# Waiting for a buffer's readers, and one addition for all deferred evictions, in a one-core hybrid trunk step

## The chip, the cores and the metric

The kernel runs as one program on one core of a Trainium2 chip. The time is the device time of one execution in microseconds (us); less is better. The engines are TensorE (PE: matmuls into eight banks of PSUM), VectorE (DVE), ScalarE (ACT), GpSimd (POOL) and SyncE (SP), whose queue issues nearly all of the DMAs.

## The reference

One inference step of a two-layer diffusion trunk over 128 context and 512 latent positions, 640 columns, with model width 2048. Each layer modulates and normalises x, multiplies by one wide input weight, runs two mixers on the halves, gates them, multiplies by an output weight and adds the result to x. The even layer has windowed attention with a sink and a gated linear scan (GLA); the odd layer has attention over a two-dimensional neighbourhood and a chunked spatial-gating MLP (gMLP).

```python
# one layer, shapes cut
m = silu(cond) @ w_ada + b_ada                 # shift, scale, gate
h = (rms_norm(x, g) * (1 + scale) + shift) @ w_in
parts = split_cols(h, SPLITS)
mix = concat(branch_a(parts), branch_b(parts)) # window attention | GLA, or 2-D attention | gMLP
x = x + gate * ((mix * silu(parts[-1])) @ w_out)
# after two layers
y = rms_norm(x, g_final)
```

All inputs and outputs are float32, and the caches and the GLA state of the context are outputs too.

## The kernel before

**Products.** Activations lie transposed, feature blocks of 128 on the partitions and 640 positions along a row, each as a high part (acth) and a low part (actl). A weight block of 128x512 is loaded as float32 into a raw buffer (wraw or rs), copied by ACT into its high half (whi, half a microsecond or so), and POOL or DVE subtracts that from the raw block to get the low half (wlo). Every product of a weight block with an activation block is three matmuls: whi with the high part, whi with the low part, wlo with the high part (`three`).

**Strassen pairs.** From the out-projection of layer 0 on, two output chunks are computed together in a pair of Winograd's form (`spair`): seven products of quarter matrices in place of eight, on sums of activations that a `fold` prepares. `fold` runs once for the odd layer's input (about 1075 to 1270 us) and once for the last out-projection (about 1900 to 2010 us), between chunks computed in the plain way. Its near half (`work`) writes the sums into SBUF as eh and el and the third operand over t3_dram; its far half (`far`) makes them in place on POOL and ACT, in Y, adas and one shared buffer `stage`, and stores them to far_dram. From there they come back as "tail" slots (`far_load`), small buffers through which the far products read them. `third` loads the third operand, t_dram in the profile, back over acth and actl when their first use is over. `keep` saves what is overwritten and `unfold` brings it back.

**Partial sums.** A product that several outputs share stays in a bank. `copy` has ACT copy it into the SBUF buffer `sums`, of which there is one, and DVE adds `sums` to each output's bank. These additions and the evictions behind them are not issued at once: `later` puts a generator into the list `evq`, and `deferred` (called by `tick`, between matmuls) takes steps of the first generator of the list when its time has come. An eviction (`ev`) first waits for flags that its chunk needs, such as home8, which is set when an attention head is done.

**What sets the order.** There is no reordering on the chip: each engine runs its instructions as they were written. The program is written by `tick`, which runs tasks (generators) between matmuls, and by a planner (`Pace`), which models when each engine and each DMA will be done. `until(...)` holds a task until the planner thinks that a buffer has been written. It doesn't ask for those who still read the buffer; if a step overwrites a buffer too soon, the engine waits on the chip for the reader's semaphore, and all that stands behind it on that engine waits too. `settle` exhausts all generators in `evq` at once, with `force` set: then no task's wait holds, and a flag that is missing is reached by running the tasks until it is there (`need`). `copy` calls it since the addition that reads `sums` has to be written before `sums` is overwritten.

**Places that the prediction names.** All ACT, DVE and POOL steps go through one helper and have line L208, all DMAs of SP L428; the matmuls have L394 (products) and L399 (transposes with ident). `tail<-bank` at 1078 us is the eviction of an output tile of layer 0 (`out_evac`), whose closing step `end` squares the tile for the norm; `Y` and `arena` are working buffers of the attention heads, and `adas` holds ada weights early and tiles of the mixers' output late.

## Time and profile before

| what | value |
| --- | --- |
| median of 3 runs | 2150.63 us (2147.55 to 2153.57) |
| the profiled execution's own time | 2151.12 us |
| its span | 2149.3 us |
| mean granted clock of PE | 0.992 |
| POOL wlo<-wraw and wlo<-rs, 128x512 | 341 of 1403 ns and 275 of 1444 ns |
| ACT whi<-wraw and whi<-rs | 397 and 329 of 623 ns |
| SP tail<-far_dram | 196 loads of 322 KB, 4.2 us to landing |

The span is the time from the first to the last instruction of the profiled execution; 1.8 us of the execution lie around it. In a row of the timeline stand the start, the length, the engine, the line, the operation, output and inputs, and in brackets how long the engine had been idle before it and what ended that. PE's idle time is what to look for, as PE is the busy engine; idle time of other engines matters where PE waits for them.

### The profile page before, as it was taken

Reading aid. Unit: us, or ns where it says so; the run is one execution under the profiler, and the core shown is the slowest. Engines: PE = TensorE matmul, PEld = TensorE weight load, DVE = VectorE, ACT = ScalarE, POOL = GpSimd, SP = SyncE. Lnnn points to the kernel's source line nnn. Section 1 sums busy time; section 2 is a strip of 40 time slices with the busy share of each in tenths; the row PEclk is TensorE's granted clock in tenths of the full one; section 3 lists DMA queues with packets and bytes.
Section 4 is the critical chain, followed back from the end, with each engine's and each line's share of the span. In section 5 each row is a group of like instructions: output and inputs, shape, how many; then the busy total and the mean of one; then the engine's idle time right before and its main releaser. Section 6 shows DMA issues by size and latency. Waiting matters only on the chain. (4 is left out here: it accounts for less than half of the span.)

```text
span 2149.3 us, 38899 instructions
## 1 busy us (share of the span) xinstructions
PE 2069.3 (96%) x13990; PEld 1985.7 (92%) x13990; DVE 1533.2 (71%) x3383; ACT 964.8 (45%) x2100; POOL 1033.0 (48%) x781
## 2 busy tenths in 40 slices
PE   7999999999999999999989999999999999999896
PEld 5789999999989999999989999999999989999896
DVE  1337777777887866788766898878778767665565
ACT  3335444343433445433554434545454544444343
POOL 3433333223313222455465666746556556656773
PEclk9999999999999999999999999999999999999998
DMA  9955333336545433866557766656666565565756
GB/s 368 324 181 162 125 106 105 104 127 189 158 119 173 141 125 102 259 217 219 156 184 243 232 217 227 230 183 212 210 216 194 189 232 194 195 222 184 242 191 218
DMA packets 216306, 412.48 MB, mean 192 GB/s; under 512 B 25712, under 2 KB 89008, under 8 KB 216112
## 3 DMA queue, kind: packets, MB, share of 16 engines
q1 hardware_dynamic: 214640, 408.43, 57.9%
q8 instruction: 110, 1.80, 0.3%
q10 hardware_dynamic: 1472, 1.56, 0.2%
q14 instruction: 84, 0.69, 0.1%
HBM read 368.83 MB, written 38.45 MB: 189 GB/s over the span
## 5 line engine op out<-in xcount | busy, mean ns | idle before, releaser
L394 PE MATMUL bank<-acth,whi 128*128 128x320 f32 (+1 forms) x3144 | 965.9, 319 | 20.9 <-ACT whi L208 8.1
L394 PE MATMUL bank<-acth,wlo 128*128 128x320 f32 (+1 forms) x3144 | 941.9, 311 | 9.7 <-POOL wlo L208 8.8
L394 PE MATMUL bank<-actl,whi 128*128 128x320 f32 (+1 forms) x3144 | 939.2, 310 | 0.0
L208 POOL TENSOR_TENSOR wlo<-wraw,whi 128x512 fp32r<-128x512 f32 x345 | 480.3, 1399 | 749.5 <-ACT whi L208 648.3
L394 PEld LDWEIGHTS bank<-acth,whi 128*128 128x128 f32 x3144 | 584.5, 189 | 41.2 <-ACT whi L208 10.8
L394 PEld LDWEIGHTS bank<-acth,wlo 128*128 128x128 f32 x3144 | 584.1, 189 | 14.8 <-POOL wlo L208 13.2
L394 PEld LDWEIGHTS bank<-actl,whi 128*128 128x128 f32 x3144 | 584.7, 189 | 1.5
L208 POOL TENSOR_TENSOR wlo<-rs,whi 128x512 fp32r<-128x512 f32 x275 | 393.4, 1444 | 238.3 <-ACT whi L208 196.4
L208 ACT ACTIVATE whi<-wraw 128x512 fp32r<-128x512 f32 (+1 forms) x397 | 242.6, 623 | 161.3 <-PE bank L394 84.5
L208 ACT ACTIVATE whi<-rs 128x512 fp32r<-128x512 f32 x329 | 197.6, 623 | 57.9 <-PE bank L394 35.3
L208 DVE CUSTOM_DVE_ANT_0 adas<-adas,bank,partg 128x256 bf16<-128x256 f32 (+1 forms) x320 | 178.1, 557 | 14.8 <-DMA adas<-ada_g 5.0
L394 PE MATMUL bank<-tail,whi 128*128 128x322 f32 (+1 forms) x672 | 152.5, 314 | 6.6 <-DMA tail<-far_dram 6.5
L394 PE MATMUL bank<-eh,whi 128*128 128x322 f32 (+1 forms) x444 | 139.8, 315 | 0.0
L394 PE MATMUL bank<-eh,wlo 128*128 128x322 f32 (+1 forms) x444 | 138.5, 312 | 1.0 <-POOL wlo L208 1.0
L394 PE MATMUL bank<-el,whi 128*128 128x322 f32 (+1 forms) x444 | 138.0, 311 | 0.0
L208 ACT ACTIVATE bc<-bank 128x2 f32<-128x2 f32 (+1 forms) x101 | 17.2, 170 | 230.9 <-DVE arena L208 153.6
L394 PEld LDWEIGHTS bank<-tail,whi 128*128 128x128 f32 x672 | 112.5, 189 | 7.4 <-DMA tail<-far_dram 7.4
L208 ACT ACTIVATE Y<-bank 128x128 f32<-128x128 f32 (+5 forms) x134 | 52.6, 412 | 140.2 <-PE bank L394 82.2
L394 PE MATMUL bank<-tail,wlo 128*128 128x322 f32 (+1 forms) x336 | 104.4, 311 | 0.2 <-POOL wlo L208 0.2
L208 DVE TENSOR_TENSOR bank<-bank,sums 128x320 f32<-128x320 f32 (+1 forms) x162 | 76.5, 493 | 36.7 <-PE bank L394 28.9
L208 ACT ACTIVATE arena<-arena,bc 128x192 f32<-128x192 f32 (+4 forms) x167 | 82.3, 517 | 42.6 <-DVE arena L208 40.9
L208 DVE TENSOR_TENSOR rs<-rs 128x512 f32<-128x512 f32 x83 | 84.4, 1025 | 21.2 <-POOL wlo L208 20.5
(215 smaller groups left out, 2928.1 us busy)
## 6 DMA issues: line engine op xcount, KB each, us to landing
tail<-far_dram SPq DMA_DIRECT2D x196, 322.0 KB, 4.2
wraw<-w_even SPq DMA_DIRECT2D x176, 256.0 KB, 3.3
adas<-ada_g SPq DMA_DIRECT2D x128, 256.0 KB, 4.2
adas<-ada SPq DMA_DIRECT2D x128, 256.0 KB, 3.6
rs<-w_odd SPq DMA_DIRECT2D x63, 512.0 KB, 5.4
Y<-ada SPq DMA_DIRECT2D x37, 512.0 KB, 5.8
wraw<-w_odd SPq DMA_DIRECT2D x37, 512.0 KB, 5.4
rs<-w_out SPq DMA_DIRECT2D x30, 512.0 KB, 5.0
```

The lines of the kernel that those rows point to most:

```text
L208: return f(*args, **kw)
L394: self.nc.tensor.matmul(out, lhsT, rhs, start=start, stop=stop, **kw)
```

## The change

Three edits, all to when a step is written and none to what it computes.

1. `clear` now asks the planner when the engine could run a step that writes `outs` and reads `ins`, readers of `outs` included, and holds the task until that is no more than 0.1 us ahead, and until no DMA that the planner holds for late touches them. It is called before the ACT copy of the near half's split (new) and of the far half's split (before: without the engine and with a looser rule), before the closing step of an output tile (before: `until`) and before the scaling of Y's tiles (`scales`).
2. `copy`, and the step of a plain block that starts the output ya, call `release` in place of `settle`. The list `xq` holds the deferred generators that still have to read `sums`; `release` forces each of them up to its addition (`used_up` takes it off the list), and what follows, the eviction, stays deferred.
3. `third` waits, ahead of its first far block, until the tail slots have been loaded.

```diff
-    def clear(self, *aps):
-
-        spans = [self.pace.span(x) for x in aps]
-        while not self.force and (self.left(*aps) > 0.05 or any(self.pace.meet(x[1], spans) for x in self.pace.late)):
-            yield 0.5
+    def clear(self, e, outs, ins=()):
+
+        pc = self.pace
+        o, i = [pc.span(x) for x in outs], [pc.span(x) for x in ins]
+        while not self.force:
+            if any(pc.meet(x[1], o) or pc.meet(x[1][:1], i) for x in pc.late):
+                yield 0.5
+                continue
+            w = pc.ready(e, o, i) - self.now
+            if w <= 0.1:
+                return
+            yield w
...
+    def release(self):
+
+        while self.xq:
+            item = self.xq[0]
+            was, self.force, self.busy = (self.force, self.busy), True, True
+            try:
+                next(item[1])
+            except StopIteration:
+                self.evq.remove(item)
+            self.force, self.busy = was
...
         def copy(a):
-            self.settle()
+            self.release()
             x = self.sums[:, : a.shape[1]]
             nc.scalar.activation(x, a, AF.Copy)
             return x
...
-        def later(c, gen):
+        def later(c, gen, x=True):
             self.evq.append([self.now, gen, c])
+            if x:
+                self.xq.append(self.evq[-1])
+
+        def used_up():
+            self.xq.pop(0)
+            yield
 
         def one(xa, x):
             yield from self.until(x)
             plus(full(xa), x)
+            yield from used_up()
             yield from ev(c1, xa, None)
             self.drop(xa)
...
                     ya = ya or take()
-                    self.settle()
+                    self.release()
                     plain(key, ya, v)
...
         def split(h, l, p):
+            yield from self.clear("a", [h], [p])
             nc.scalar.activation(h, p, AF.Copy)
...
-                yield from self.clear(h, x)
+                yield from self.clear('a', [h], [x])
                 h, l = h.bitcast(F32R), x.bitcast(F32R)
...
                 yield from self.wait("Tn" if i < NR else "Tf", f"{used if i < NR else far_used}:{i}")
+                if i == NR:
+                    yield from self.until(*self.slots)
                 for n, x in enumerate((self.ah, self.al)):
...
             def end(c):
-                yield from self.until(y[:, c], self.sq)
+                yield from self.clear('a', [self.sq], [y[:, c]])
                 square(y, c)
...
-                yield from self.clear(Y[:, k, :])
+                yield from self.clear('a', [Y[:, k, :]])
```

The numbers of instructions are the same on every engine but for 16 subtractions wlo that move from DVE to POOL. PE's order is the same up to about 1095 us (in the first fold); after that only small matmuls (attention, transposes, sums over partitions) and a few plain blocks stand elsewhere between the weight products.

**ACT in the second fold (about 1926 to 1942 us).** Before; Y<-Y, Y<-adas and stage<-adas are the far half's copies, arena<-Y is a step of the gates, whi the weights' high halves:

```order
L208 ACTIVATE Y<-Y 128x320
L208 ACTIVATE stage_7782<-adas 128x320
L208 ACTIVATE whi<-rs_7781 128x512 x2
L208 ACTIVATE Y<-adas 128x320
L208 ACTIVATE stage_7782<-adas 128x320
L208 ACTIVATE arena_7788<-Y 128x320 x4
L208 ACTIVATE sums_7784<-bank_69 128x320
L208 ACTIVATE whi<-wraw 128x512 x2
L208 ACTIVATE whi<-rs_7781 128x512 x2
```

And with the change, the rows that stand there:

```order
L208 ACTIVATE stage_7782<-adas 128x320
L208 ACTIVATE whi<-rs_7781 128x512
L208 ACTIVATE Y<-Y 128x320
L208 ACTIVATE whi<-wraw 128x512
L208 ACTIVATE arena_7788<-Y 128x320 x2
L208 ACTIVATE whi<-wraw 128x512
L208 ACTIVATE arena_7788<-Y 128x320 x2
L208 ACTIVATE stage_7782<-adas 128x320
L208 ACTIVATE sums_7784<-bank_70 128x320
L208 ACTIVATE whi<-rs_7781 128x512
L208 ACTIVATE Y<-adas 128x320
```

The two weight copies whi<-wraw stood behind both overwriting steps with adas, the four gate steps and the copy into sums; one of them now stands ahead of the gate steps and one between them, and the step Y<-adas that followed the first stage<-adas stands behind them all.

**PE at the end of attention head 7 (1726 us).** The bank that PE's products with Y write is filled from transposes (ident). Before:

```order
L399 MATMUL bank_72<-ident,Y 128x128 x3
L399 MATMUL bank_73<-ident,arena_7788 128x128
L399 MATMUL bank_73<-ident,arena_7788 64x128
L399 MATMUL bank_73<-ident,arena_7788 128x128
L394 MATMUL bank_72<-Y 128x512
L394 MATMUL bank_72<-Y 128x128
L394 MATMUL bank_72<-Y 128x256 x3
L394 MATMUL bank_72<-Y 128x128
L394 MATMUL bank_69<-acth,whi 128x320
L394 MATMUL bank_69<-actl,whi 128x320
L394 MATMUL bank_69<-acth,wlo 128x320
```

With the change, the two places, first behind the first transposes, then ahead of the products with Y (the rows between are weight products like those shown):

```order
L399 MATMUL bank_72<-ident,Y 128x128 x3
L394 MATMUL bank_69<-acth,whi 128x320
L394 MATMUL bank_69<-actl,whi 128x320
L394 MATMUL bank_69<-acth,wlo 128x320
L394 MATMUL bank_69<-acth,whi 128x320
```

```order
L399 MATMUL bank_73<-ident,arena_7788 128x128
L399 MATMUL bank_73<-ident,arena_7788 64x128
L399 MATMUL bank_73<-ident,arena_7788 128x128
L394 MATMUL bank_71<-eh_7779,whi 128x322
L394 MATMUL bank_71<-el_7780,whi 128x322
L394 MATMUL bank_71<-eh_7779,wlo 128x322
L394 MATMUL bank_71<-eh_7779,whi 128x322
```

The second group of transposes stood directly behind the first and the products with Y directly behind the second; now 18 weight products stand between the two groups, and 18 between the second group and the products with Y.

**SP at the end of the second fold (about 1990 to 2007 us).** Before:

```order
L428 DMA tail_19307<-far_dram 128x2x320
L428 DMA acth<-t_dram 128x320
L428 DMA actl<-t_dram 128x320
L428 DMA arena_7788<-x1T_dram 128x640
L428 DMA acth<-t_dram 128x320
L428 DMA actl<-t_dram 128x320
L428 DMA acth<-t_dram 128x320
L428 DMA actl<-t_dram 128x320
L428 DMA arena_7788<-x1T_dram 128x640
L428 DMA tail_19307<-far_dram 128x2x320 x5
```

With the change:

```order
L428 DMA far_dram<-tail_18201 128x320 x2
L428 DMA tail_19165<-far_dram 128x2x320 x3
L428 DMA rs_7781<-w_out 128x1024
L428 DMA tail_19165<-far_dram 128x2x320
L428 DMA wraw<-w_out 128x1024
L428 DMA acth<-t_dram 128x320
L428 DMA actl<-t_dram 128x320
L428 DMA acth<-t_dram 128x320
L428 DMA actl<-t_dram 128x320
```

Before, the first row is the third load of the tail slots, and the fourth, in the last row, stood behind loads of t_dram over acth and actl and two of x1T_dram; with the change four tail loads stand ahead of the first load of t_dram.

More of the change, by code (lines that the diff above doesn't have):

```diff
@@ L256, in __init__ @@
         self.folded = self.quiet = False
-        self.inline, self.evq, self.lows, self.chunk_no = True, [], [], 0
+        self.inline, self.evq, self.lows, self.chunk_no, self.xq = True, [], [], 0, []
         self.room = self.rooms[0]
@@ L1055, in two @@
             plus(x, y)
+            self.xq.pop(0)
         def three_(xb, x):
@@ L1059, in three_ @@
             plus(half(xb), x)
+            yield from used_up()
             yield from ev(c1, None, half(xb))
@@ L1066, in four @@
             plus(half(v), half(x))
+            yield from used_up()
             yield from ev(c2, ya, None)
@@ L1075, in five @@
             nc.vector.tensor_tensor(half(xb), half(xb), half(x), ALU.subtract)
+            yield from used_up()
             yield from ev(c2, ya, None)
@@ L1081, in six @@
             plus(half(xb), x)
+            yield from used_up()
             yield from ev(c1, None, half(xb))
@@ L1118, in spair @@
                     later(c1, six(xb, x))
-                    later(c2, seven(t))
+                    later(c2, seven(t), False)
             elif f == "S1":
```

## The prediction

> **What bounds the kernel now.** I read the page's span and busy times first, then its slices, then a table by stage, and last TensorE's own timeline around each of its gaps.
>
> ```profile
> span 2149.3 us, 38899 instructions
> PE 2069.3 (96%) x13990; PEld 1985.7 (92%) x13990; DVE 1533.2 (71%) x3383; ACT 964.8 (45%) x2100; POOL 1033.0 (48%) x781
> PE   7999999999999999999989999999999999999896
> PEclk9999999999999999999999999999999999999998
> 1700.00:1740.00 40.00, 35.36 (x215) 31.95 (x214) 28.19 (x74) 21.15 (x47) 18.24 (x14) 0.96 0.51 168
> 1900.00:2010.00 110.00, 99.12 (x641) 97.78 (x640) 60.42 (x91) 44.56 (x94) 74.91 (x66) 0.95 0.68 223
> ```
>
> TensorE (PE) is busy 2069.3 of 2149.3 us and the next engine, VectorE (DVE), 71%. The change neither adds nor drops an instruction, so PE's work stays and only two things can go: the 80.0 us in which PE is idle, and the time that it runs below full clock. The table by stage (PE, weight load, DVE, ACT, POOL, granted clock, DMA share, GB/s) finds both at a few places: 11 us idle at 0.95 clock in the 110 us of the second fold, 4.6 us at 0.96 in the 40 us around 1720. The first 850 us of the program aren't touched by the order of the change, and their idle time stays.
>
> What PE waited for between 850 and 2010 us (total, times, longest), and the four stalls that stick out, with the granted clock of the stretch behind each (the column ahead of the DMA share):
>
> ```profile
> PE bank L394 <- POOL wlo L208: 7.6, 14, 0.8
> PE bank L394 <- ACT whi L208: 7.2, 6, 3.9
> PE bank L394 <- DMA tail<-far_dram: 6.5, 2, 5.1
> PE bank L394 <- DVE arena L208: 4.3, 5, 1.3
> 1082.16 0.78 PE L394 MATMUL bank<-acth,whi 128*128 128x322 f32 x2 [3.92 <-DVE tail L208]
> 1729.60 0.55 PE L399 MATMUL bank<-ident,arena 128*128 128x128 f32 x3 [2.90 <-DVE arena L208]
> 1731.09 1.49 PE L394 MATMUL bank<-Y 128*128 128x512 f32 x2 [0.94 <-ACT Y L208]
> 1941.14 0.63 PE L394 MATMUL bank<-acth,whi 128*128 128x320 f32 x1 [3.93 <-ACT whi L208]
> 2005.32 0.90 PE L394 MATMUL bank<-tail,whi 128*128 128x320 f32 x2 [5.14 <-DMA tail<-far_dram]
> 1082.10:1086.67 4.57, 4.51 (x18) 4.33 (x19) 1.42 (x4) 1.63 (x4) 2.61 (x3) 0.63 0.58 217
> 1731.00:1736.00 5.00, 4.91 (x12) 2.82 (x12) 1.16 (x7) 0.04 (x1) 0.00 (x0) 0.66 0.31 120
> 1941.10:1946.81 5.71, 5.67 (x21) 5.44 (x21) 5.69 (x5) 3.07 (x6) 4.69 (x5) 0.50 0.19 65
> 2005.30:2008.33 3.03, 3.01 (x11) 3.02 (x12) 0.00 (x0) 0.63 (x1) 1.41 (x2) 0.52 0.60 172
> ```
>
> The gaps are 3.92, 2.90 + 0.94 = 3.84, 3.93 and 5.14 us, 16.83 together. Behind each the clock is granted at 0.50 to 0.66 for 3 to 6 us; what that costs is length times missing share: 4.57 x 0.37 = 1.7, 5.00 x 0.34 = 1.7, 5.71 x 0.50 = 2.9, 3.03 x 0.48 = 1.5, together 7.8. So four stalls hold 24.6 us, more than all other waits of PE that the change can reach.
>
> [...]
>
> **The change part by part.** *Waiting until a buffer's readers are done.* The second fold shows what the old order does on ScalarE (ACT):
>
> ```profile
> 1935.94 0.47 ACT L208 ACTIVATE Y<-adas 128x320 fp32r<-128x320 f32 x1 [7.52 <-DMA far_dram<-Y]
> 1937.26 0.47 ACT L208 ACTIVATE stage<-adas 128x320 fp32r<-128x320 f32 x1 [0.85 <-DMA far_dram<-stage]
> 1937.64 1.17 ACT L208 ACTIVATE arena<-Y 128x320 f32<-128x320 f32 x3
> 1939.78 0.47 ACT L208 ACTIVATE arena<-Y 128x320 f32<-128x320 f32 x1 [0.97 <-POOL arena L208]
> 1940.15 0.42 ACT L208 ACTIVATE sums<-bank 128x320 f32<-128x320 f32 x1
> 1940.47 1.14 ACT L208 ACTIVATE whi<-wraw 128x512 fp32r<-128x512 f32 x2
> ```
>
> The fold's step was queued while the store of its buffer was still under way, so ACT stood 7.52 us, and the weight copies behind it (whi<-wraw at 1940.47) came late; PE's 3.93 us is the end of that. In the order of the change two whi<-wraw stand ahead of the step Y<-adas and of the second stage<-adas; of the ACT steps that overwrite a buffer less than 20 matmuls behind the store that reads it, 30 in the second half before, 7 are left. **Second fold: 3.93 + 2.9 = 6.8 us, of which I take 6.3**; bounds 0 (the whi waits for something else) and 6.8. Nothing here is added: the step itself is the same 0.47 us, and its far products come hundreds of matmuls later.
>
> At the first fold's entry (1082) PE waited for evictions of output tiles behind a chain of ACT and DVE steps that the closing step of each eviction held up. The change queues the first eviction 5 to 8 matmuls earlier, but the second stands right at the product that needs its bank. The nearest rows for such an eviction wait are those of the second fold's entry:
>
> ```profile
> 1902.74 0.42 PE L394 MATMUL bank<-acth,whi 128*128 128x320 f32 x1 [1.29 <-DVE arena L208]
> 1906.17 0.41 PE L394 MATMUL bank<-acth,whi 128*128 128x320 f32 x1 [0.51 <-DVE arena L208]
> ```
>
> Two of them cost 1.29 + 0.51 = 1.8, no clock lost: **3.92 + 1.7 - 1.8 = 3.8 us**; bounds 0 and 5.6.
>
> *Releasing one addition only.* At 1726 the copy of a partial sum forced every deferred eviction out, one of which needed the flag of attention head 7; the planner then ran that head to its end with nothing between its steps. PE's rows show it: transposes, 2.90 us, transposes, 0.94 us, the products with Y. In the new order 18 weight products stand between the two transposes and 18 between those and the products with Y, some 18 x 0.145 = 2.6 us of cover each (0.145 from the rows in which two matmuls start 0.29 apart, below). **5.5 us are at stake, I take 4.5**, since the DVE and ACT steps of the head still have to fit; bounds 0 and 5.5.
>
> ```profile
> 1077.50 0.45 PE L394 MATMUL bank<-actl,whi 128*128 128x320 f32 x2
> 1077.79 0.45 PE L394 MATMUL bank<-acth,wlo 128*128 128x320 f32 x2
> ```
>
> *Waiting for the tail slots.* On SP's queue before, loads for the third products stood among those of the tail:
>
> ```profile
> 1995.40 4.29 DMA acth<-t_dram
> 1999.70 5.57 DMA tail<-far_dram
> ```
>
> These are links of the chain of waits: the tail load issued at 1999.70 had to wait for the landing of acth<-t_dram, issued at 1995.40, took 5.57 us, and PE stood until 2005.32. Now four tail loads stand ahead of the first acth and actl load, and the first is queued some 80 matmuls (12 us) earlier because the far steps end earlier. **5.14 + 1.5 = 6.6, I take 6.0**; bounds 0 and 6.6. What is held back, acth and actl, feeds the third products, which run behind the tail products and are covered by them; without that cover the price is one load, 4.29 us by the row above.
>
> *Small waits.* Without the four stalls 7.6 (POOL wlo) + 3.3 (ACT whi) + 1.4 (tail) = 12.3 us of the same kind stay, weight copies that come late. The order has the worst of them further ahead of their products, but not all. I take half, **6.1**; bounds 0 and 12.3.
>
> *Moved and added.* 16 subtractions wlo go from DVE to GpSimd (POOL):
>
> ```profile
> L208 POOL TENSOR_TENSOR wlo<-wraw,whi 128x512 fp32r<-128x512 f32 x341 | 476.3, 1403 | 741.9 <-ACT whi L208 640.7 <-PE bank L394 31.0 <-PE bank L399 22.0
> L208 DVE TENSOR_TENSOR wlo<-wraw,whi 128x512 fp32r<-128x512 f32 x52 | 59.5, 1148 | 52.0 <-ACT whi L208 47.5 <-POOL tail L208 2.3 <-POOL arena L208 1.7
> ```
>
> 1403 for 1148 ns: 0.26 us each, on an engine idle half the time; hidden at nothing by the products that stand between, and at most 16 x 0.8 (the longest wlo wait) = 12.8 us if every one came last. [...]
>
> New tight places in the order: three attention steps Y<-bank stand two matmuls ahead of their reader (0.94 each by the row at 1731.09) and two wlo on POOL ten ahead (0.8 each): **4.4 us against**; bounds 0 and, with the moved subtractions, 17.
>
> **Sum**: 6.3 + 3.8 + 4.5 + 6.0 + 6.1 - 4.4 = 22.3 us. It is made against the profiled execution, whose own time is 2151.12 us (span 2149.3), 0.5 above the median of the runs, 2150.63. 2151.1 - 22.3 = **2128.8 us**, said as 2129.
>
> **The rivals.** *Only the two waits of the second fold go* (6.3 + 6.0 = 12.3, 2139 us): the forced head and the small waits come back elsewhere, since DVE, at 28.19 of 40 us around 1720, still has the same chain to run. For it: the first fold's second eviction, which stands as tight as before. Against it: the 18 and 18 products put between.
>
> *The stalls only move* (2151, no change): the planner's model of when a store lands is wrong by more than its new margin of 0.1 us, and ACT stands as long as before, at another row. For it: the two loads of the chain above took 4.29 and 5.57 us, so a landing is not one number. Against it: the rule now counts late stores, and the whi stand ahead of the step whatever the store takes.
>
> *Slower*: what isn't forced is left in the queue and keeps its banks. 125 copies of partial sums stand in the program, and each cleared the queue before:
>
> ```profile
> L208 ACT ACTIVATE sums<-bank 128x320 f32<-128x320 f32 (+1 forms) x125 | 53.9, 431 | 69.8 <-PE bank L394 69.1
> ```
>
> If PE then waits for a bank at the next product, at 1.29 us (the row at 1902.74), 17 such waits (21.9) eat the 22.3 us, from there on it is slower: 25 of the 125 give 32.3 - 22.3 = 10 us more, 2161, and 40 give 51.6 - 22.3 = 29, 2180. Against it: in the order no product starts on a bank whose eviction stands less than a few matmuls ahead, except at the places named.
>
> *The change doesn't do what it says*: nothing moves where it counts. The order speaks against it.
>
> **How the numbers follow.** Forecast 0.57; only the second fold 0.23; stalls only move 0.12; slower 0.06; nothing done 0.02. The forecast's own bounds run from all small waits gone and no new ones (22.3 + 6.1 + 4.4 = 32.8, so 2118) to half the gain (2140). The range, 2117 to 2146, holds the forecast and the second fold's case with half of its gain gone too, 0.8 together; the rest is left out. A change under 0.3%, 6.5 us, can't be told from none by a measurement of this kernel: faster 0.82, same 0.12, slower 0.06.
>
> **What would show it.** Right: no PE gap above 2 us between 1080 and 2010, a granted clock of 1.00 in the two stages quoted first, and ACT without a wait of 7 us for far_dram<-Y ahead of a weight copy. Wrong step by step: a gap at the first fold's entry as long as 3.9 (evictions), a gap with head 7's transposes (release), tail<-far_dram still at 5 us (slots). Rival: many PE waits of 1 us for DVE's arena or rs at the start of a chunk, or wlo waits on POOL well above 7.6 us.

## The result and the profile after

| | before | with the change |
| --- | --- | --- |
| median | 2152.1 us (4 runs, 2147.55 to 2154.49) | 2113.64 us (4 runs, 2111.34 to 2116.72) |
| ratio | | 0.9825, 95% interval 0.9803 to 0.9846 |
| profiled execution, its span | 2151.12, 2149.3 us | 2111.34, 2109.6 us |

The change makes the kernel 38 us faster where 22 were forecast, and 2113.6 lies below the range, which began at 2117. Two executions of the runs below, one of the kernel without the release (9165.53 us) and one of the kernel before (5168.41 us), were in a slow state and are left out of every median. The page of the changed kernel, the lines that answer to those of before:

```profile
span 2109.6 us, 38920 instructions
PE 2054.4 (97%) x13990; PEld 1978.4 (94%) x13990; DVE 1518.0 (72%) x3367; ACT 970.3 (46%) x2100; POOL 1047.1 (50%) x797
PE   7999999999999999999999999999999999999996
PEclk9999999999999999999999999999999999999998
1675.90:1714.20 38.30, 38.30 (x265) 38.13 (x265) 29.48 (x60) 21.98 (x47) 24.18 (x17) 1.00 0.69 229
1875.00:1971.40 96.40, 94.31 (x637) 93.56 (x636) 62.64 (x93) 44.66 (x93) 75.35 (x63) 1.00 0.77 248
```

Of the two stages in which PE stood before, the end of attention head 7 is full now (38.30 of 38.30 us) and the last fold all but full (94.31 of 96.40), both at a clock of 1.00. PE's idle time falls from 80.0 to 2109.6 - 2054.4 = 55.2 us, 24.8 less; and PE's busy time, with the same 13990 matmuls, falls by 14.9. The second number is the part that a list of gaps doesn't show: matmuls at half clock (15.3 us of PE's busy time between 850 and 2050 before, none with the change), and longer ones behind a wait (0.41 us for 0.31, last section). What PE waited for between the events that lay at 850 and 2010 before:

```profile
PE bank L394 <- DVE arena L208: 3.5, 4, 1.3
PE bank L394 <- POOL wlo L208: 3.3, 6, 0.8
PE bank L394 <- DVE tail L208: 3.2, 2, 1.9
PE bank L394 <- ACT whi L208: 0.8, 2, 0.4
1073.78 0.78 PE L394 MATMUL bank<-acth,whi 128*128 128x322 f32 x2 [1.24 <-DVE tail L208]
1078.87 0.78 PE L394 MATMUL bank<-acth,whi 128*128 128x322 f32 x2 [1.94 <-DVE tail L208]
```

No wait for tail<-far_dram is left, whi and wlo went from 14.8 to 4.1 us, and the longest wait of all is the 1.94 us of the second output tile at the odd layer's fold. On ACT the overwriting steps of the last fold wait far less for the store to far_dram (1.3 us in all for far_dram<-Y, 0.6 at most, where it was 10.9 and 7.5), and the weight copies stand between them:

```profile
1909.74 0.47 ACT L208 ACTIVATE arena<-Y 128x320 f32<-128x320 f32 x1 [1.81 <-POOL arena L208]
1910.12 0.46 ACT L208 ACTIVATE stage<-adas 128x320 fp32r<-128x320 f32 x1
1910.48 0.42 ACT L208 ACTIVATE sums<-bank 128x320 f32<-128x320 f32 x1
1910.80 0.62 ACT L208 ACTIVATE whi<-rs 128x512 fp32r<-128x512 f32 x1
1911.85 0.47 ACT L208 ACTIVATE Y<-adas 128x320 fp32r<-128x320 f32 x1 [0.43 <-DMA far_dram<-Y]
```

**Where the time went.** The order of the weight products on PE hardly changes, so the same weight matmul (the nth that reads whi or wlo) can be found in every trace, and the time between two of them compared. The stretches are named by their time in the kernel before; a number is the time that a profiled execution took there, less that of before; the first stretch begins at the first weight matmul and the last ends at the last one, so that the sum of the change is 38.5 where the spans differ by 39.7. PE's order is the same in all these kernels up to about 1085 us, so the first row, with up to 2.2 us, shows what executions differ by. Behind that a few small matmuls stand in another stretch than before: with the change 15 fewer in the odd layer's fold, 13 more in the pairs and 2 more in head 7's. "Calm" are two kernels with one number of the planner moved, explained below.

| stretch (us before) | change | plumbing | calm before | calm after | only clear | only release | only third |
| --- | --- | --- | --- | --- | --- | --- | --- |
| 0 to 940 | -0.4 | -0.2 | -1.3 | -1.6 | -0.4 | -2.2 | -1.8 |
| out-projection, to 1070 | -4.4 | -2.7 | -3.2 | -4.4 | -4.4 | -4.5 | -1.9 |
| entry of the odd layer's fold, to 1090 | -1.8 | +1.8 | -1.4 | +0.5 | -1.6 | -0.8 | +0.5 |
| that fold, to 1190 | -7.6 | +0.1 | +5.0 | -7.7 | -6.0 | +1.2 | +0.1 |
| pairs, to 1700 | -4.3 | -0.1 | +0.1 | -3.3 | -0.7 | +0.4 | -3.7 |
| head 7, to 1750 | -7.2 | +0.7 | +0.8 | -5.8 | -1.0 | -5.8 | +2.8 |
| to 1935 | +1.5 | 0.0 | +2.4 | +2.6 | +3.2 | +1.7 | +0.1 |
| whi in the last fold, to 1945 | -6.1 | +0.5 | -5.7 | -6.1 | -6.1 | -0.3 | -0.4 |
| to 1995 | -0.7 | -0.4 | +0.2 | -0.7 | -0.7 | 0.0 | -0.7 |
| tail slots, to 2010 | -6.7 | +1.9 | +5.9 | -6.7 | -6.7 | -6.7 | -5.4 |
| third products, to 2050 | 0.0 | 0.0 | 0.0 | +0.1 | 0.0 | 0.0 | +2.1 |
| to the end | -0.7 | -2.1 | -1.3 | -0.3 | +3.1 | -1.1 | -1.4 |
| sum | -38.5 | -0.5 | +1.5 | -33.7 | -21.4 | -18.1 | -9.6 |

| stretch | no release | no third | calm, no release | calm, no third | no work | work late | no far | no scales | no end |
| --- | --- | --- | --- | --- | --- | --- | --- | --- | --- |
| out-projection | -4.4 | -4.4 | -4.4 | -4.4 | -4.4 | -4.4 | -4.4 | -4.0 | -4.4 |
| entry | -1.6 | -0.6 | 0.0 | -0.3 | -5.0 | -4.6 | -2.0 | +0.8 | -1.9 |
| odd layer's fold | -7.7 | -4.9 | -7.4 | -3.9 | -3.4 | -1.9 | -0.9 | -7.7 | -7.6 |
| pairs | -3.2 | -2.5 | -2.0 | -2.0 | -3.7 | -3.3 | +2.7 | -0.4 | -3.5 |
| head 7 | +0.4 | -2.3 | -0.3 | -4.3 | -5.8 | -4.3 | -4.3 | -5.9 | -7.2 |
| whi, last fold | -6.1 | -6.1 | -6.1 | -6.1 | -6.1 | -6.1 | -6.1 | -6.1 | -6.1 |
| to 1995 | -0.7 | -0.7 | -0.7 | -0.7 | -0.7 | -0.7 | +6.0 | -0.7 | -0.7 |
| tail slots | -6.7 | -6.7 | -6.7 | -6.7 | -5.8 | -6.7 | -6.7 | -6.7 | -6.7 |
| third products | +0.8 | 0.0 | +0.8 | 0.0 | +8.1 | 0.0 | 0.0 | 0.0 | 0.0 |
| sum, all stretches | -26.3 | -26.5 | -24.2 | -24.3 | -27.0 | -30.6 | -17.4 | -26.6 | -34.9 |

The four stalls that the forecast named give 1.8 + 7.2 + 6.1 + 6.7 = 21.8 us; it had 20.6. The other 16.7 us lie outside them, where the forecast's sum had 6.1 - 4.4 = 1.7.

### The profile page after: what moved, and what is told of

The parts are those of the page before. It is cut to its first block, busy times and chain, and to the rows that moved or that the text cites. A ratio compares the mean times of both kernels' runs of the same rounds, so it can differ in the third digit from the quotient of the medians.

```text
span 2109.6 us, 38920 instructions
## 1 busy us (share of the span) xinstructions
PE 2054.4 (97%) x13990; PEld 1978.4 (94%) x13990; DVE 1518.0 (72%) x3367; ACT 970.3 (46%) x2100; POOL 1047.1 (50%) x797
## 5 line engine op out<-in xcount | busy, mean ns | idle before, releaser
L208 POOL TENSOR_TENSOR wlo<-rs,whi 128x512 fp32r<-128x512 f32 x285 | 401.7, 1421 | 217.8 <-ACT whi L208 193.0
L208 ACT ACTIVATE bc<-bank 128x2 f32<-128x2 f32 (+1 forms) x101 | 17.2, 170 | 230.4 <-DVE arena L208 148.1
L208 DVE TENSOR_TENSOR rs<-rs 128x512 f32<-128x512 f32 x83 | 89.2, 1085 | 26.7 <-POOL wlo L208 26.4
```

The costliest lines, as they stand in the source:

```text
L208: return f(*args, **kw)
```

## The experiments

Each kernel is the changed one with the edit shown, unless said otherwise. The first line of a result is its median and its ratio to the kernel before on the same chip, with the 95% interval.

**One edit taken back.** Without the release:

```diff
         def copy(a):
-            self.release()
+            self.settle()
```

> The change without its second edit: copy and the step ya exhaust all deferred evictions again. Theory 1 (each edit owns the stalls that its rows name): the order has the forced attention head back at about 1700 us, transposes and products with Y directly behind each other; PE stands there for about 3.8 us and runs a window of 3.4 us at half clock, 1.7 more; everything else as with the change: 2113.6 + 5.5 to 6 = about 2119.5. Theory 2 (the gain beyond the forecast is the releasing: evictions that are not forced leave DVE and ACT free for the weight halves, so the small waits went with it): the small waits of 5 to 13 us come back as well, 2125 to 2133.

2123.68 us, 0.9871 (0.9836 to 0.9905). By the stretches theory 1: the stall is back at its place, with its half clock, and the odd layer's fold keeps its -7.7. The time lies between the two theories. PE's timeline at the end of head 7, and the table by stretches of the time behind it, where the clock is 0.69:

```profile
1709.36 0.55 PE L399 MATMUL bank<-ident,Y 128*128 128x128 f32 x3 [0.56 <-DVE Y L208]
1713.00 0.87 PE L399 MATMUL bank<-ident,arena 128*128 128x128 f32 x3 [3.10 <-DVE arena L208]
1714.82 2.08 PE L394 MATMUL bank<-Y 128*128 128x512 f32 x2 [0.94 <-ACT Y L208]
1714.80:1721.60 6.80, 6.78 (x22) 4.31 (x23) 0.00 (x0) 1.32 (x3) 0.00 (x0) 0.69 0.11 31
```

The stretch costs 7.6 us more than with the change, above the 5.5 to 6 expected: gaps of 0.56 + 3.10 + 0.94 = 4.6, the clock with 6.80 x 0.31 = 2.1, where I had reckoned 1.7, and 0.27 for each gap that its bracket doesn't hold (the last section), together 7.5. Of the other 4.6 us in the sums, 1.1 lie in the pairs and 2.4 behind 2050, without a mechanism that I could show.

Without the wait of the third operand:

```diff
-                if i == NR:
-                    yield from self.until(*self.slots)
```

> The change without its third edit: the third operand's loads no longer wait for the tail slots. Theory 1 as I forecast it (this edit owns the stall of 5.14 us at 2000): the stall is back with its half clock, +6.6 us, 2120. Rival (the far steps end earlier by the first edit, so the tail loads are far enough ahead anyway): in the order the tail loads of the last fold stand exactly as with the change, no stall for tail<-far_dram; only four small tight places more between 1350 and 1700 (weight copies 0 to 11 matmuls ahead), 1 to 2 us each: 2116 to 2120, and none of it at the last fold.

2125.84 us, 0.9881 (0.9854 to 0.9908), 23.9 us below before where the change has 38.5. At the last fold nothing changes (-6.7 stays), so my step is wrong and the rival right there; but the cost is above the rival's, and partly at the odd layer's fold, which I hadn't looked at. PE's timeline there, and at 1700:

```profile
1175.68 0.56 PE L394 MATMUL bank<-tail,whi 128*128 128x322 f32 x2 [0.80 <-DMA tail<-far_dram]
1700.64 0.41 PE L394 MATMUL bank<-acth,whi 128*128 128x322 f32 x1 [1.74 <-ACT whi L208]
1701.99 0.64 PE L394 MATMUL bank<-acth,wlo 128*128 128x322 f32 x1 [0.80 <-POOL wlo L208]
```

Without the near half's wait, and without that of the far half (its old form):

```diff
         def split(h, l, p):
-            yield from self.clear("a", [h], [p])
             nc.scalar.activation(h, p, AF.Copy)
```

> The change without the wait in the near half's split. Theory 1: the first fold's entry is as before, 3.9 us and half clock for the 1.2 + 1.9 that the change leaves, +2.5 to 4; and in the order of the last fold the loads acth<-t_dram stand 0 to 6 matmuls ahead of their products, so PE stands there for about one load, 4 to 5 us, with 1.7 us of half clock: +6. Together 2121 to 2124. Rival (the entry's stall belongs to the closing step of an output tile, as I forecast): no change at the entry, 2119.

2129.46 us, 0.9897 (0.9871 to 0.9923), above both theories. The profiled execution took 2124.06 us, so its column holds 5.4 us less than the median lost. The wait for acth<-t_dram came as the order said, 1.94 and 2.97 us in two rows, and the third products took 8.1 us longer. At the entry it is the other way round: PE waits 0.36 us there, not the 3.9 that were expected; the near half's wait costs 3.2 us at the entry and brings 4.2 in the fold behind.

```profile
1072.35 0.78 PE L394 MATMUL bank<-acth,whi 128*128 128x322 f32 x2 [0.36 <-DVE tail L208]
1986.08 0.41 PE L394 MATMUL bank<-acth,whi 128*128 128x320 f32 x1 [1.94 <-DMA acth<-t_dram]
1990.05 0.63 PE L394 MATMUL bank<-acth,whi 128*128 128x320 f32 x1 [2.97 <-DMA acth<-t_dram]
```

```diff
-                yield from self.clear('a', [h], [x])
+                yield from self.clear0(h, x)   # clear as it was before
                 h, l = h.bitcast(F32R), x.bitcast(F32R)
```

> The change with the old, looser wait in the far half's split. Theory 1 (the far half's overwriting owns the 3.9 us stall for whi at 1937): ACT stands for stores again, 19 of its steps stand less than 20 matmuls behind a store; the stall for whi comes back, +6.8 us, and in the first part of the last fold acth<-t_dram stands 3 to 6 matmuls ahead, PE 4 us and half clock, +5 more: 2125. Rival (the near half's wait alone moves the weight copies out of the way): in the order the whi that came last before stands far ahead, so no 3.9 us for whi; only the wait for acth<-t_dram, +5 to 6: 2119.

2132.55 us, 0.992 (0.9894 to 0.9945), the dearest edit to take back. The rival is right about the 3.9 us for whi: it doesn't come back (-6.1), as either half's wait is enough for that. What comes back is in the odd layer's fold, -0.9 for -7.6, in the pairs, +2.7 for -4.3, and around the loads of the last fold. This is how one wait of the odd layer's fold is made, ACT's timeline first; the last row is PE's:

```profile
1109.96 0.47 ACT L208 ACTIVATE Y<-tail 128x320 fp32r<-128x320 f32 x1 [3.90 <-DMA far_dram<-Y]
1114.24 0.47 ACT L208 ACTIVATE stage<-Y 128x320 fp32r<-128x320 f32 x1 [3.48 <-DMA far_dram<-stage]
1114.62 0.61 ACT L208 ACTIVATE whi<-wraw 128x512 fp32r<-128x512 f32 x1
1943.44 0.38 PE L394 MATMUL bank<-acth,whi 128*128 128x320 f32 x1 [2.61 <-DMA acth<-t_dram]
```

ACT stands 3.48 us for a store of stage, the weight copy queued behind it starts at 1114.62, and PE, in its list of waits from 1090 to 1190, has 1.4 us for whi. The last row is the wait for acth<-t_dram in the last fold, +6.7 with the half clock behind it (a matmul with wlo takes 0.47 us at 1946.16, 0.31 ahead of the wait). In the pairs the longest wait for whi, 1.28 us at 1322, is of another make: the copy stands behind an attention step (bc<-bank) for which ACT waited 6.82 us for DVE, not for a store.

Without the wait ahead of the scaling, and without that ahead of an output tile's closing step (both in their old form):

```diff
-                yield from self.clear('a', [Y[:, k, :]])
+                yield from self.clear0(Y[:, k, :])
```

> The change with the old, looser wait ahead of the scaling of Y's tiles. Theory 1 (that wait alone keeps ACT from standing for x1T_dram<-Y during the out-projection of layer 0, and PE's small waits for whi there are nothing but that): ACT's waits for x1T_dram<-Y, 3.9 us with the change, are back near the 38.6 us of before, and the stretch from 940 to 1070 us takes 4.4 us longer again; one weight copy more is tight at about 1710: 2118 to 2121. Rival (small waits are a matter of how the order happens to fall, and any change of it would have removed them): that stretch stays as with the change, 2112 to 2116.

2120.12 us, 0.9857 (0.9836 to 0.9878): the time that theory 1 expected, for another reason. ACT's waits for x1T_dram<-Y are back, and yet the out-projection stays at -4.0. Theory 1 falls there: those waits had cover. What the profiled execution loses stands elsewhere, 2.6 us at an entry with a gap of 3.88, the stall of before, which no other edit brings back when it alone is taken back, 3.9 in the pairs and 4.8 behind 2050; it was the slowest of its four (2124.38), so the median holds about half of that.

```profile
ACT Y L208 <- DMA x1T_dram<-Y: 34.3, 10, 6.3
1076.15 0.78 PE L394 MATMUL bank<-acth,whi 128*128 128x322 f32 x2 [3.88 <-DVE tail L208]
```

```diff
             def end(c):
-                yield from self.clear('a', [self.sq], [y[:, c]])
+                yield from self.until(y[:, c], self.sq)
```

> The change with the old wait ahead of the closing step of an output tile. In the order all tight places are those of the change. Theory 1: this edit is worth nothing, 2112 to 2117 with the two waits of 1.2 and 1.9 us at the first fold's entry as they are. Rival, as I forecast it (this edit moved the evictions at the first fold's entry ahead): a gap of 3.9 us with half clock there, 2116 to 2118.

2111.29 us, 0.9818 (0.9798 to 0.9838). Theory 1: it is worth nothing, and the entry is as with the change (-1.9 for -1.8). The eviction that I credited to this edit moves with the wait ahead of the scaling (3.88 us without it) and with the near half's (0.36 without it).

**One edit alone**, with the other two taken back as above.

> The kernel before with the second edit alone. Theory 1 (local): the forced head at 1726 is gone, -7; the tail loads of the last fold stand 47 and more matmuls ahead (7 us) where the last one stood 3, so the stall at 2000 is gone too, -6.6; the 3.9 us for whi at 1937 and its half clock stay, and so do all small waits of the out-projection and of the first fold: about 2136. Rival (the stall at 2000 belongs to the third edit): only the head goes, 2143. If the releasing were what removed the small waits, 2120 to 2125.

2134.95 us, 0.9929 (0.9906 to 0.9952). Theory 1: the head and the tail slots go, -5.8 and -6.7, and whi at 1937 stays; the small waits of the odd layer's fold stay too (+1.2). Only the out-projection, which was to stay, gives 4.5.

```profile
1931.11 0.63 PE L394 MATMUL bank<-acth,whi 128*128 128x320 f32 x1 [3.61 <-ACT whi L208]
```

> The kernel before with the third edit alone. As I forecast it: the stall at 2000 goes, -6.0, 2144. Rival (it trades one wait for another): the tail loads stand 31 matmuls ahead, but the loads acth<-t_dram that are held back stand 9 to 31 matmuls ahead of their products, 1.3 to 4.6 us where one takes 4.3; PE waits there for 3 to 5 us and loses the clock again: no gain, 2147 to 2152.

2143.83 us, 0.9964 (0.9953 to 0.9976). The time is that of my forecast, and the mechanism half that of the rival: the wait for the tail slots shrinks from 5.14 to 1.04 us, and 0.90 us for acth<-t_dram appears behind it (-5.4, then +2.1).

```profile
1994.98 0.57 PE L394 MATMUL bank<-tail,whi 128*128 128x320 f32 x2 [1.04 <-DMA tail<-far_dram]
2008.86 0.41 PE L394 MATMUL bank<-acth,whi 128*128 128x320 f32 x1 [0.90 <-DMA acth<-t_dram]
```

> The first edit alone, in all four places. Theory 1: the stalls at 1937 and 2000 and the small waits of the first fold are gone (-13 and -7), the forced head stays (+7.6 against the change), and the order has four weight copies 0 to 4 matmuls ahead between 1100 and 1710, 1.5 to 2 us each with their wlo: 2124 to 2130. Rival (the third edit is needed for the stall at 2000): 6 more, 2131 to 2136.

2126.47 us, 0.9887 (0.987 to 0.9903). Theory 1: whi and tail slots at -6.1 and -6.7 without the third edit, the fold at -6.0, head 7 at -1.0 for -7.2. The first edit carries two thirds of the gain.

**The order moved by something else.** Is the gain between the stalls the change's, or does any new order bring it? One number of the planner, in the kernel before and in the changed one:

```diff
-    rooms, calms, lags = (0.3, 1.2, 1.5, 0.8), (4.0, 2.0), (3.0, 3.0, 2.0, 1.0, 0.4)
+    rooms, calms, lags = (0.3, 1.2, 1.5, 0.8), (3.6, 1.7), (3.0, 3.0, 2.0, 1.0, 0.4)
```

> The kernel before with one number of the planner moved that has nothing to do with the change (calms, how far DVE may be behind before a fold step is put off, from 4.0 and 2.0 to 3.6 and 1.7). Theory 1 (the stalls have mechanisms that the change removes): the forced head at 1726 and the small waits of the first fold (1090 to 1190) stay; the stall for whi at 1937 falls away by chance of the order, where no weight copy is tight there any more: 2138 to 2147. Theory 2 (the gain of the change is mostly the order falling otherwise, and any such move would give it): 2125 or less.

2153.16 us, 1.0011 (1.0002 to 1.0021). Theory 2 falls outright, and theory 1's time too: the 3.9 us for whi at 1937 did go (-5.7), but others took its place. An addition that reads the sums now stops PE in the odd layer's fold (+5.0). Around the tail slots (+5.9) 4.95 us of wait stand as before; new are 2.80 and 0.63 us ahead of them, and the matmuls with wlo take 0.47 us from 1997.84 to 2006.63, where they took 0.31 at 1994.19; before, the clock was at half here for 3.41 us:

```profile
1161.23 0.64 PE L394 MATMUL bank<-acth,whi 128*128 128x320 f32 x1 [5.19 <-DVE sums L208]
2005.93 0.90 PE L394 MATMUL bank<-tail,whi 128*128 128x320 f32 x2 [4.95 <-DMA tail<-far_dram]
```

> The changed kernel with the same number moved. Theory 1: the gain stays with the change: in the order one weight copy (whi, 0 matmuls ahead) is tight at about 1700 us and nothing else new, +2 to 4 us with its wlo: 2114 to 2119, 22 to 30 below the kernel before with the same number. Theory 2: small waits come back all over, 2125 or more, and the two moved kernels differ by less than 15.

2115.55 us, 0.9831 (0.9816 to 0.9847). Theory 1: with the number moved the change brings 37.6 us by the medians, against 38.5 without. So the gain is the change's, though single stalls of the kernel before come and go with the order.

The changed kernel with all three edits taken back, only the list xq and its extra yield left:

> The changed kernel with all three edits taken back, only the list xq and its extra yield left. The order is that of before but for some 60 matmuls elsewhere. Both theories: as before, 2148 to 2153, the four stalls and the small waits where they were; what differs by stretch shows what a run or so small a move of the order is worth.

2151.55 us, 0.9999 (0.9988 to 1.001). As before. By the program's names (buffer numbers left out) its trace has the same operations in the same order on all five engines as that of before, so its column shows about what two executions differ by: up to 2.7 us in a stretch. Those 2.7 lie in the out-projection. There the kernels without the first two edits lose 1.9 to 3.2, all others 4.0 to 4.5, so of the change's 4.4 us only about 1 to 2.5 can be credited to it.

> The moved planner number, without the third edit; to compare with calm_after, 2115.6. Theory 1 (with the first edit in, the third is worth nothing, and the 12 us that no_third cost were chance of the order between the folds): 2113 to 2120. Rival (it is worth its 12 us): 2125 to 2130.

2123.62 us, 0.9877 (0.9849 to 0.9906), 8.1 us above calm after and 9.4 by the table, between what the two theories expected. Some of it is the edit's, in the odd layer's fold (-3.9 for -7.7), and SP's timeline shows how. Without the edit, with PE's wait in the last row, then with it:

```profile
1163.95 1.27 SPq L428 DMA_DIRECT2D tail<-far_dram  x3
1165.32 0.38 SPq L428 DMA_DIRECT2D acth<-t_dram  x1
...
1169.61 0.38 SPq L428 DMA_DIRECT2D actl<-t_dram  x1
1170.05 0.42 SPq L428 DMA_DIRECT2D tail<-far_dram  x1
1175.78 0.56 PE L394 MATMUL bank<-tail,whi 128*128 128x322 f32 x2 [2.51 <-DMA tail<-far_dram]
```

```profile
1162.78 1.27 SPq L428 DMA_DIRECT2D tail<-far_dram  x3
1164.15 0.38 SPq L428 DMA_DIRECT2D adas<-ada_g  x1
1164.58 0.47 SPq L428 DMA_DIRECT2D tail<-far_dram  x1
```

The fourth load of the tail slots is issued 5.5 us later behind the loads over acth and actl, and PE waits 2.51 us for it. It is the mechanism that I described for the last fold, at the other fold. What is left lies mostly in the pairs (1.3), in head 7's stretch (1.5) and behind 2050 (2.4), without a mechanism that I could show.

> The moved planner number, without the second edit. Theory 1 (the forced head is a mechanism, and costs about 7.5 us with its half clock in any order): PE stands between head 7's transposes again, 2122 to 2128. Rival (chance, as with the third): within 4 us of calm_after, 2112 to 2119.

2125.86 us, 0.9892 (0.9868 to 0.9916). Theory 1: head 7 at -0.3 for -5.8, in another order as well.

The near half's wait in the last fold alone:

```diff
-            yield from self.clear("a", [h], [p])
+            if self.folded or yt0:   # yt0: yt was given, the last fold
+                yield from self.clear("a", [h], [p])
```

> The change with the near half's wait in the last fold alone. Theory 1 (the wait is worth 8 us in the last fold, where it keeps acth<-t_dram from coming late, and in the odd layer's fold it takes about as much at the entry as it gives behind it): the entry's two waits of 1.2 and 1.9 become one of about 0.4, the stretch from 1090 to 1190 loses 4 us, no wait for acth<-t_dram at 1985: 2113 to 2119. Rival (the wait matters in the odd layer's fold above all): 2122 to 2128, as without it.

2119.24 us, 0.9858 (0.9831 to 0.9885). The stretches are theory 1's: no wait for acth<-t_dram, the entry at -4.6, the fold behind at -1.9; it loses 5.7 and gains 2.8, so the wait is better in both folds.

No version beats the change beyond the spread: leaving out the closing step's edit gives 2111.29 for 2113.64, with intervals that overlap.

## Why the prediction was too small

The signs that it named for being right all came: the longest PE gap is 1.94 us, the clock is 1.00 in both stages, and ACT's longest wait for far_dram<-Y in the last fold is 0.6 us. The sum was too small, and the step that failed is its term for the small waits together with the one for new ones.

- **Second fold, whi at 1937 (6.3 forecast):** right, 6.1. Either half's wait is enough, by the two runs without one of them.
- **Releasing one addition (4.5):** right in place and mechanism, too small: 7.2 in the stretch to 1750, and 7.6 and 5.5 by the two runs without it. I had left 1 us for what wouldn't be hidden; all was, and a small wait for wlo in that stretch went too.
- **Tail slots (6.0):** right in size, 6.7, wrong in cause. It needn't the third edit: the first alone and the second alone give the same -6.7, since the far steps end earlier: the last store to far_dram is issued 7.8 us ahead of the first tail product before, 22.6 with the first edit alone and 13.1 with the second. I had that as a side remark ("the first is queued some 80 matmuls (12 us) earlier") and should have seen that it suffices. The third edit works at the odd layer's fold.
- **First fold's entry (3.8):** too large, 1.8, and put to the wrong place: the closing step's edit is worth nothing, and the stall comes back without the wait ahead of the scaling. The two waits that are left are 1.24 + 1.94 for the 1.29 + 0.51 that I borrowed from another place; the near half's wait makes most of them. The 1.8 is no more than the stretch's spread (+1.8 with the plumbing alone, +0.5 in calm after).
- **Small waits (6.1) and new ones (-4.4):** the step that failed; 16.7 us came from there, not 1.7. The rows of before that I left out of the list:

```profile
PE bank L394 <- ACT Y L208: 1.9, 2, 0.9
PE bank L394 <- DVE sums L208: 0.8, 1, 0.8
PE bank L394 <- DVE wlo L208: 0.7, 1, 0.7
```

Four things add up to most of it. Of the 12.3 us for whi, wlo and the tail, 8.2 went (3.3 + 0.8 are left), not half; 0.8 of them is in head 7's stretch and counted there: 1.3 more. Waits that I hadn't put on the list went nearly all: DVE sums 0.8, DVE wlo 0.7, the half of ACT Y that isn't head 7's, 0.9, and 0.7 of DVE arena (4.3 less two pairs of gate evictions at 1.29 + 0.51), 3.1; with the 0.5 for bc and Y that are new, 2.6. Of the five new tight places the three attention steps show no wait, and those for wlo, if they wait, are within the 3.3 that are left: 4.4. And every wait that goes takes about 0.27 us with it that stands in no bracket (below); PE's gaps above 0.2 us between 900 and 2060 went from 31 to 15, of which the four stalls are 5 and 2, so 13 x 0.27 = 3.5. Together 11.8 of the 15.0 that were missing.

Counted directly, without the forecast's terms, the gain closes better. Between 940 and 2050 us the kernel became 37.4 us shorter. PE's gaps above 0.2 us went from 34.7 to 10.4, which is 24.3; PE was busy at half clock for 15.3 us and now isn't at all, which is 7.7 (the forecast had 7.8); and 16 gaps fewer at 0.27 are 4.3. That is 36.3. So the clock's price was right, and what the forecast missed are gaps and the time that a gap costs beyond its length.

- **Why the small waits went:** some of them in the odd layer's fold are the same mechanism as the large ones, an overwriting step of the fold ahead of a weight copy. The run without the far half's wait shows one, and ACT's timeline before another, 2.84 us for a second store lying between these rows; PE then waits 0.36 us for that whi at 1140.3:

```profile
1135.96 0.47 ACT L208 ACTIVATE stage<-Y 128x320 fp32r<-128x320 f32 x1 [8.46 <-DMA t_dram<-stage]
1139.65 0.61 ACT L208 ACTIVATE whi<-wraw 128x512 fp32r<-128x512 f32 x1
```

Not all are: the 0.88 us for whi at 1103 stands behind a norm step (rstd<-arena) for which ACT waited 4.99 us for DVE, and why those of that kind went as well isn't shown. I took half since the order moved not all of them; I should have followed each of them back to the ACT row ahead of it, and asked whether the change moves that one.

- **The rivals:** nothing of the slower one was seen: the evictions that stay in the queue hold no bank that PE waits for. DVE's arena, the row that would show it, is at 3.5 us for 4.3, and the two pairs of gate evictions are all of that. The 16 subtractions on POOL cost nothing that can be seen, wlo's waits fell from 7.6 to 3.3 us. In the chances, "nothing done" (0.02) was counted as faster; it belongs to the same, which makes 0.80 and 0.14.

No run moves those subtractions alone, so what they cost by themselves isn't shown; POOL's mean for wlo<-wraw of 128x512 is 1386 ns for 1403.

The parts don't add up. Against the kernel before on the same chip, the runs without one part keep 26.1 (release), 23.9 (third), 20.3 (near half), 17.2 (far half), 32.8 (scaling) and 41.6 (closing step) of the 38.5 us, so that the parts would cost 69.1 together; alone, the edits give 25.4 (first), 18.0 (second) and 9.1 (third), 52.5. The tail slots are counted three times among those that stand alone, and each kernel has an order of its own between the folds: the pairs' stretch runs from -4.3 to +2.7. A correction to the part ahead: `fold` also runs a third time, first of all and without a far half, for the out-projection of layer 0; nothing above rests on it.

## What to carry to other kernels

Where an engine runs its steps in the order in which they are written, as ACT does here (its 1994 ACTIVATE rows in the trace of before stand as in the program), hold a step until the readers of what it overwrites are done, not only until its inputs are there: the store it waits for, 7.5 us in the last fold before, also delays everything behind it, here the weight copies of the busiest engine. To price such a change, go through the small waits too, and follow each back to the row on the other engine that held it up; here some stood behind an overwriting step and others behind a step that waited for another engine. And judge a new order by a second one: with one number moved, single stalls of the kernel before came and went without any change in its total.

## What the hardware showed

**What a wait cost beyond its bracket.** PE's timeline before, at two small waits; the first column is the start:

```profile
1023.01 0.31 PE L394 MATMUL bank<-actl,whi 128*128 128x320 f32 x1
1023.16 0.31 PE L394 MATMUL bank<-acth,wlo 128*128 128x320 f32 x1
1023.82 0.41 PE L394 MATMUL bank<-acth,whi 128*128 128x320 f32 x1 [0.36 <-ACT whi L208]
1024.08 0.30 PE L394 MATMUL bank<-actl,whi 128*128 128x320 f32 x1
1025.23 0.41 PE L394 MATMUL bank<-acth,wlo 128*128 128x320 f32 x1 [0.85 <-POOL wlo L208]
1025.48 0.31 PE L394 MATMUL bank<-acth,whi 128*128 128x320 f32 x1
```

Starts are 0.15 us apart. Over the wait of 0.36 they are 1023.82 - 1023.16 = 0.66 apart, 0.51 too much, and the next 0.26, 0.11 too much: 0.62 lost for 0.36. Ahead of the wait the rows overlap, 0.31 us long and 0.15 apart; that the difference is this overlap, emptied by the wait and filled again, is my reading and isn't shown. Over 22 such waits of 0.25 to 2.2 us at full clock in this trace the difference has a median of 0.27, over 17 in that of the change the same.

**Where the clock was at half.** Between 100 and 2090 us the trace of before has the clock granted at 0.50 for 6.83 us from 598.50, 3.41 from 1083.19, 3.41 from 1731.72, 6.83 from 1939.94 and 3.41 from 2004.79, that of the change for 6.83 from 596.62 alone. The later starts lie 142, 332, 393 and 412 times 3.413 us behind the first. Cut in such steps from the first start, these two traces have 575 and 580 pieces at full clock: the six that lie ahead of a stretch at half clock hold 2.03 to 3.41 us of PE idle, the others at most 1.62. A wait of under 2 us was followed by half clock in one kernel, 3.40 x 0.49 = 1.7 us more, and not in another. The changed kernel's 1.94 us (above) and the same wait in the kernel without the third edit, with the clock of the 3.4 us behind each:

```profile
1078.90:1082.30 3.40, 3.40 (x21) 3.19 (x22) 0.28 (x1) 2.39 (x5) 2.36 (x3) 1.00 0.25 96
```

```profile
1080.28 1.00 PE L394 MATMUL bank<-acth,whi 128*128 128x322 f32 x2 [1.93 <-DVE tail L208]
1080.30:1083.70 3.40, 3.40 (x12) 3.20 (x13) 0.29 (x1) 2.39 (x5) 2.35 (x3) 0.51 0.25 96
```

21 matmuls in one case, 12 in the other, for the same wait. With the change one of the steps, at 1077.90, parts the 1.94 us into 0.97 and 0.97; how they lie in the other trace isn't shown.
